# A later lead for the preparation of x, a shorter root for single tiles, and tile 0's root ahead of the weight maxima

## The chip, the cores and the metric

The kernel runs on one core of one Trainium2 chip. The metric is the device time of one execution in microseconds (us); the time shown is the median of three. The core has five engines that work at the same time, each through its own instructions in order: TensorE (PE in the rows; its weight loads are PEld), VectorE (DVE), ScalarE (ACT), GpSimd (POOL) and SyncE (SP), which here only issues DMAs. They wait for each other through semaphores.

## What is computed

One layer of a hybrid encoder over x of 2048 x 1024 (float32):

```
hn = rms_norm(h, norm_w)
proj = hn @ w_in.astype(jnp.float32)
u_f, g_f, q, k, v, g_a = jnp.split(proj, SPLIT_POINTS, axis=-1)
...
f = jnp.fft.fft2(u_f, axes=(1, 3), norm="ortho").real.astype(jnp.float32)
...
o_c, lse_c = dilated_window_attention(q[:, :, sl], k[:, :, sl], v[:, :, sl], window, dilation, slopes)
...
mixed = jnp.concatenate([y_f, y_a], axis=-1) @ w_out.astype(jnp.float32)
h = h + mixed
```

`rms_norm` multiplies each row of x with the reciprocal root of its mean square plus 1e-6 (and with the gain norm_w, which the kernel puts into the weights). The change is in how this first line is prepared.

## The kernel before

**Number format.** Each float32 operand of the projections is split into two fp16 parts, an upper part and a lower part (the remainder). A product of x and a weight is then three products: upper with upper, lower of x with upper of the weight, upper of x with lower of the weight.

**Preparation of x.** x is handled in 16 tiles of 128 rows. Tile r goes through these steps:
- `x_load` (line 173): DMA of 512 KB, issued by SyncE, into `xs`. Tiles 0 to 11 have a place of their own; tiles 12 to 15 take the places of 6 to 9, so their loads wait until tile 6 to 9 is split.
- `x_sq` (line 189): ScalarE squares the tile and adds each row up into `xss`.
- `x_rs` (lines 193 to 200, with `rsqrt_g`, lines 104 to 111): the reciprocal root by an integer start value and three rounds of three small operations on VectorE, each waiting for the one before; 11 links with the mean. Result `xri`. Tiles 0 to 3 have a root of their own (`xn1t` is its scratch), later tiles share one root in pairs (`xn2t`), which needs both tiles' squares.
- `x_hi` (line 212): ScalarE scales the tile and casts it, the upper part (`xhl`).
- `x_lo` (line 220): VectorE computes the lower part from it (also `xhl`).
- Transposition into `xT`. The upper part: 8 transposes on TensorE (`x_tr`, line 227) into PSUM (`xps`) and one copy back (`x_ev`, line 232), on ScalarE for even tiles and on VectorE for odd ones. The lower part: for tiles 0 to 3 the same way with the engines exchanged, from tile 4 on by a DMA transpose that SyncE issues (`x_dt`, line 235).
The upper and lower parts share four buffers (`pp`), so that two tiles can be under way.

**Main loop.** It runs over items: for each of 12 units (two heads of one attention configuration) the projections of 16 tiles, later the other parts of the layer. Step i does item i. The projection of one tile (`inproj`, line 309) is 24 products of 128x128 by 128x384 into one of three PSUM buffers (`psq`); the loop issues them in pieces of 6 among the work of the other engines. The first unit goes through tiles 0 to 15 in steps 0 to 15, so tile r must be ready at step r. In the first products of every tile but tile 0, upper and lower part of x alternate, so the second product already reads the lower part. Three readers on ScalarE empty a finished projection one step later (`q_raw` and `q_v`, lines 320, 321, 328), VectorE follows with line 329 and 339.

**The order is written by hand** (a manual schedule). In step i, in this order: the DMA transposes of the tiles split in the step before (`for r in xd: ... self.x_dt(r)`), the weight loads that fall due (line 245; in steps 3 to 6 two pieces of the next unit's weights, ahead in the program of the DMA transposes of that step), the readers of the step before, the first 6 products, `x_hi` of the tiles named by `xd`, 6 products, the TensorE transposes and copies of the tiles split in the step before (`xt`), `x_lo` of the tiles in `xd` and the loads that need their places, 6 products, the squares, the rest, and at the end of some steps the rest of a root. Between these, `chain` advances by one operation the root of x (`xg`), the roots of the attention's queries and the gains (`gains`, lines 153 to 169, which ends in three DMAs). A generator that is run to its end in a `for _ in xg: pass` is issued in one piece.

**Before the loop.** All loads are issued, the weights of unit 0 first (eight pieces, `wr`); VectorE takes the absolute maximum of each piece (line 261, `w_prep`), the maxima give a power of two as scale (lines 263 to 280), ScalarE and VectorE split the weights with it (lines 286 and 288). The code interleaves `w_prep` (`wg`) with tiles 0 and 1 by `go`, which advances it by one stage.

Of the kernel before, what the change touches and what calls it, by code (L numbers as in the profile page):

```python
# [11 lines left out]
F32 = mybir.dt.float32  # L12
# [3 lines left out]
I32 = mybir.dt.int32  # L16
AF = mybir.ActivationFunctionType
OP = mybir.AluOpType
# [4 lines left out]
S, D = 2048, 1024  # L23
HD = 64
NT = 16
KT = D // 128
EPS = 1e-6
# [62 lines left out]
class Kernel:  # L90
# [100 lines left out]
    def x_rs(self, r0):  # L191
        n = self.xgrp(r0)[1]
        ss = self.XS[r0][:, :n]
        y, g = self.rsqrt_g(ss, n, "xn%d" % n, self.XR[r0][:, :n])

        def gen():
            self.nc.vector.tensor_scalar(ss, ss, 1.0 / D, EPS, op0=OP.mult, op1=OP.add)
            yield
            yield from g
        return gen()  # L200
# [747 lines left out]
    def body(self):  # L948
# [3 lines left out]
        with ExitStack() as ctx:  # L952
# [19 lines left out]
            for _ in range(2):  # L972
                t = self.stp.tile([128, 3, 2, S], F16, name="xs", tag="st", bufs=2)
# [10 lines left out]
            wg = self.w_prep(0)  # L984

            def go(*gs):
                for g in gs:
                    next(g, None)
            self.x_sq(0)
            go(wg, wg)  # L990
            for _ in self.x_rs(0):
                pass
            self.x_hi(0)
            self.x_tr(0, 0)
            go(wg, wg, wg, wg, wg, wg)
            go(wg)
            self.x_lo(0)
            self.x_ev(0, 0)
# [25 lines left out]
            xg = self.x_rs(3)  # L1024
# [32 lines left out]
            xd, xt = [], []  # L1057
            ng = og = iter(())
            self.YD, self.YL = [], []
            for i in range(max(len(items) + 1, G + 32)):  # L1060
                ip, wchunks = iter(()), 0
                if i < len(items):
                    u, _, _, gen, out = items[i]
                    ip = gen() if i else ip0
                    p = i - first[u]
                    if p == 0:
                        wg = iter(())
# [4 lines left out]
                    if p == p0 and u + 1 < NU:  # L1072
                        wg = self.w_prep(u + 1, u + 2 < NU)
# [11 lines left out]
                def chain(k=1):  # L1085
                    for _ in range(k):
                        next(og1, None)
                        next(ng, None)
                        next(xg, None)
                        if 0 < i < NT:  # L1090
                            next(kg, None)
# [26 lines left out]
                if q4:  # L1118
                    self.q_st(*q4)
                chain(1)  # L1120
                xd = [r for r in ([i + 2] if i < 2 else [4, 5] if i == 2 else [i + 3]) if r < NT]
                next(ip, None)
                if b0:
                    self.att_exp(*b0)
# [39 lines left out]
                        self.x_load(r + 6)  # L1164
                chain(2)
                next(ip, None)
                if i < 2:
                    self.x_sq(2 * i + 4)
                    self.x_sq(2 * i + 5)
                elif i + 6 < NT:  # L1170
                    self.x_sq(i + 6)
                chain(1)
                for _ in range(wchunks):
                    next(wg, None)
# [5 lines left out]
                    self.att_o(*ao3)  # L1180
                for _ in og1:
                    pass
                if i % 2 == 0 or i == 1:
                    for _ in xg:
                        pass
                if i == 0:
                    xg = self.x_rs(4)
                if i % 2 and i + 6 < NT:
                    xg = self.x_rs(i + 5)
                if p == count[u] - 1:  # L1190
                    for _ in wg:
                        pass
# [104 lines left out]
```

## Time and profile before

| | |
|---|---|
| time, median of 3 | 1406.22 us |
| lowest and highest of the three | 1406.18 and 1406.72 us |
| time of the profiled execution | 1406.38 us |
| its span, first to last instruction | 1404.6 us |
| mean granted TensorE clock | 0.997 |
| busy: TensorE, VectorE, ScalarE, GpSimd | 98%, 71%, 53%, 33% |

Rows of a timeline have the start of a run of like instructions, its length, engine, line, operation, output and input, the count behind the x, and in brackets how long the engine stood idle ahead of it and what ended that. A length includes the latency of the last instruction, so the pace of a run is better read from starts. In a list of waits a row has who waited for whom, the sum, how many times, and the longest. In the chain of waits a row has the start, the length and what the end of the program waited for at that time.

### The profile page before, as it was taken

To read this page: it belongs to the slowest core of one execution; us is meant where nothing else is said; L and a number is where in the kernel's file an instruction comes from. 1 tells how busy PE (TensorE), PEld (TensorE's weight loads), DVE (VectorE), ACT (ScalarE), POOL (GpSimd) and SP (SyncE) were. 2 spreads that over 40 slices of the span, in tenths; PEclk is the share of its full clock that TensorE was granted. 3 is DMA by queue.
4 is the path that set the end of the run, shared out by engine and by line. 5 is a ranking of instruction groups with operands and counts; after the bars stand their busy time and mean duration, and the time that the engine had idled before them with its cause. 6 is when DMAs were issued, how large, how long until landed. Compare 5 with 4: busy or idle time off the path is not lost.

```text
span 1404.6 us, 27759 instructions
## 1 busy us (share of the span) xinstructions
PE 1373.1 (98%) x9484; PEld 1018.3 (72%) x9484; DVE 996.0 (71%) x3174; ACT 748.9 (53%) x2101; POOL 462.6 (33%) x639
## 2 busy tenths in 40 slices
PE   5999999999999999999999999999999999899998
PEld 3666666667777777778888888844447689688887
DVE  7888888887878888888887777754398877721111
ACT  6867767676766666675756565645213335410010
POOL 0265444444444444454543343321000100411110
PEclk9999999999999999999999999999999999999999
DMA  6977777777776877687766565544423527364342
GB/s 225 205 133 122 153 123 144 124 145 132 138 137 120 151 119 158 116 153 120 142 116 125 103 131 109 128 110 132 168 83 101 155 83 255 91 158 128 112 112 83
DMA packets 426686, 187.62 MB, mean 134 GB/s; under 512 B 320112, under 2 KB 410416, under 8 KB 426032
## 3 DMA queue, kind: packets, MB, share of 16 engines
q1 hardware_dynamic: 397940, 172.84, 56.9%
q10 hardware_dynamic: 28604, 13.00, 4.0%
q8 instruction: 74, 1.21, 0.4%
q14 instruction: 68, 0.56, 0.1%
HBM read 67.65 MB, written 29.76 MB: 69 GB/s over the span
## 4 chain that ended last, share of the span: by engine, by line
PE 82%; DVE 6%; DMA 4%; issue 3%; POOL 2%; ACT 2%; SPq 1%; ACTq 0%; POOLq 0%; DVEq 0%
PE psq L309 44%; PE py L937 13%; PE psq L571 12%; PE psq L587 5%; PE pS L458 3%; PE po L524 2%; PE po L525 1%; DMA Y<-SG 1%; PE pS L446 1%; DVE xhl L220 1%; POOL ph L506 1%; DMA wor<-in_w_out_dram 1%; DMA qw<-qw 1%; DVE wh L288 0%; DMA pt<-ph 0%
## 5 line engine op out<-in xcount | busy, mean ns | idle before, releaser
L309 PE MATMUL psq<-wh,xT 128*128 128x384 f16 x4608 | 787.4, 327 | 3.3 <-ACT wh L286 1.5
L309 PEld LDWEIGHTS <-xT 128*128 128x128 f16 x4608 | 540.6, 119 | 193.9 <-issue 5.1
L494 ACT ACTIVATE P<-pS,ob,kb 128x256 f32<-128x256 f32 (+1 forms) x384 | 199.7, 527 | 150.8 <-DVE ob L486 150.4
L506 POOL TENSOR_TENSOR ph<-P,ph 128x512 f16<-128x512 f32 x160 | 189.3, 1183 | 195.6 <-ACT ph L501 183.3
L937 PE MATMUL py<-wo,mx 128*128 128x512 f32 x768 | 176.5, 392 | 5.9 <-DVE mx L916 4.8
L362 POOL TENSOR_TENSOR qn<-qn,kb 128x128 f32<-128x128 f32 x192 | 85.1, 443 | 294.0 <-DVE qn L361 202.8
L937 PEld LDWEIGHTS py<-wo,mx 128*128 128x128 f32 x768 | 145.4, 190 | 37.1 <-DVE mx L916 5.2
L571 PE MATMUL psq<-xT,wh 128*128 128x512 f16 x768 | 169.0, 379 | 0.0
L476 DVE CUSTOM_DVE_ANT_0 pS<-pS,bt 128x256 f32<-128x256 f32 (+1 forms) x384 | 147.8, 385 | 27.1 <-PE pS L446 18.8
L373 POOL TENSOR_TENSOR hl<-qn,hl 128x256 f16<-128x256 f32 x192 | 134.3, 699 | 30.6 <-ACT hl L368 30.6
L571 PEld LDWEIGHTS <-wh 128*128 128x128 f16 x768 | 74.1, 98 | 87.1 <-issue 0.8
L940 DVE TENSOR_TENSOR xo<-xo,py 128x512 f32<-128x512 f32 x32 | 22.0, 688 | 139.6 <-PE py L937 139.6
L535 DVE TENSOR_REDUCE ob<-po 128x128 f32<-128x256 f32 (+1 forms) x160 | 75.2, 470 | 53.9 <-PE po L525 53.9
L501 ACT CAST ph<-P 128x512 f16<-128x512 f32 x160 | 99.1, 619 | 8.7 <-DMA wr<-in_w_in_dram 1.7
L368 ACT CAST hl<-qn 128x256 f16<-128x256 f32 x192 | 77.1, 401 | 47.3 <-POOL qn L362 37.5
L329 DVE TENSOR_TENSOR vt<-psq,vt 128x128 f16<-128x128 f32 x192 | 55.0, 286 | 60.7 <-ACT vt L328 60.6
L328 ACT CAST vt<-psq 128x128 f16<-128x128 f32 x192 | 51.3, 267 | 82.9 <-PE po L525 82.9
L288 DVE SCALAR_TENSOR_TENSOR wh<-wr,nws,wh 128x384 f16<-128x384 f32 x128 | 87.5, 690 | 7.1 <-ACT wh L286 7.1
L587 PE MATMUL psq<-wh,xT 128*128 128x256 f16 x768 | 84.3, 273 | 0.0
L587 PEld LDWEIGHTS <-xT 128*128 128x128 f16 x768 | 75.1, 98 | 9.1
L915 ACT CAST mx<-ya 128x512 fp32r<-128x512 f16 x16 | 9.9, 620 | 134.5 <-PE py L937 127.8
L320 ACT COPY raw<-psq 128x256 f32<-128x256 f32 x192 | 69.6, 362 | 21.6 <-PE psq L309 21.2
(158 smaller groups left out, 1770.8 us busy)
## 6 DMA issues: line engine op xcount, KB each, us to landing
wr<-in_w_in_dram SPq DMA_DIRECT2D x104, 192.0 KB, 3.0
ot<-O SPq DMA_DIRECT2D x16, 792.0 KB, 4.6
st<-st SPq DMA_DIRECT2D x96, 128.0 KB, 2.4
xs<-in_x_dram SPq DMA_DIRECT2D x16, 512.0 KB, 7.2
xo<-in_x_dram SPq DMA_DIRECT2D x16, 512.0 KB, 3.7
out_dram<-xo SPq DMA_DIRECT2D x15, 512.0 KB, 3.0
O<-ob ACTq DMA_DIRECT2D x108, 66.0 KB, 2.6
O<-ob ACTq DMA_DIRECT2D x32, 132.0 KB, 3.1
```

Of the source, the lines that this page charges most:

```text
L288: V.scalar_tensor_tensor(wh[:, 1, k - 1, :n], wr[k - 1], nws[:, k - 1:k], wh[:, 0, k - 1, :n], op0=OP.mult, op1=OP.subtract)
L309: nc.tensor.matmul(ps[:, :384], self.xtile(j, k, c, t), wh[:, l, k, :384], start=n == 0, stop=n == 23)
L362: G.tensor_tensor(qn[:, 2:4], qn[:, 2:4], self.kf[:, h0:h0 + 2], OP.mult)
L368: self.nc.scalar.copy(hl.rearrange("p a h l d -> p (a h) l d")[:, :, 0], qn)
L373: self.nc.gpsimd.tensor_tensor(hv[:, :, 1], qn, hv[:, :, 0], OP.subtract)
L476: V.tensor_tensor_reduce(out=sS[:, h, cs], in0=ps[:, h, cs], in1=bs, scale=1.0, scalar=-3.0e38, op0=OP.add, op1=OP.max, accum_out=mx[:, e, ...
L494: self.nc.scalar.activation(P[:, h, cs], sS[:, h, cs], AF.Exp, bias=ob[:, e, 130 + h:131 + h], scale=self.om[:, h0 + h:h0 + h + 1], accum_ ...
L501: self.nc.scalar.copy(ph[:, 0], P)
L506: self.nc.gpsimd.tensor_tensor(ph[:, 1], P, ph[:, 0], OP.subtract)
L571: nc.tensor.matmul(ps, wh[:, l, k, col * 128:col * 128 + 128], self.xT[:, j, k, ch * 512:ch * 512 + 512], start=n == 0, stop=n == 23)
L587: nc.tensor.matmul(ps[:, j * 256:j * 256 + 256], self.xT[:, i, k, r * 128:r * 128 + 128], wh[:, l, k, 128:384], start=n % 24 == 0, stop=n ...
L937: nc.tensor.matmul(ps[nh], m[:, j, k], wo[nh][k][:, l], start=(j, l, k) == (0, 0, 4), stop=(j, k) == (1, 3))
```

## The change

1. **A root of its own form for single tiles.** `x_rs` of tiles 0 to 3 takes the mean with a factor of -1/2 in the first operation, a start value for that, and then three rounds of two operations instead of three: 8 links instead of 11. The roots of pairs keep their form.
2. **Tile 0's root ahead of the maxima.** Before the loop, two maxima stood between the square and the root of tile 0; they now follow it with the other six.
3. **The lead.** Which tiles are split in step i (`xd`) was tile 2 in step 0, tile 3 in step 1, tiles 4 and 5 in step 2 and tile i + 3 from then on. Now it is tile i + 2 in steps 0 to 3, tiles 6 and 7 in step 4 and tile i + 3 from then on.
4. **The squares** were two a step in steps 0 and 1 (tiles 4 to 7) and one a step from then on (tile i + 6). Now they are one a step in steps 0 to 3 (tile i + 4), two in steps 4 and 5 (tiles 8 to 11), and tile i + 6 from then on.
5. **The roots of pairs.** The root of 4 and 5 was spread over step 1 (from the end of step 0, with the rest in one piece at its end). Now the roots of 4 and 5, 6 and 7, 8 and 9 are issued in one piece at the end of steps 1, 3 and 4; that of 10 and 11 is spread from step 5 on as before.

```diff
@@ x_rs
+        if n == 1:
+            y = self.XR[r0][:, :1]
+            t = self.sm.tile([128, 1], F32, name="xnt", bufs=3)
+
+            def gen1():
+                V.tensor_scalar(ss, ss, -0.5 / D, -0.5 * EPS, op0=OP.mult, op1=OP.add)
+                yield
+                V.tensor_scalar(y.bitcast(I32), ss.bitcast(I32), -0.5, float(0x5F3759DF - 2 ** 30 - 2 ** 22), op0=OP.mult, op1=OP.add)
+                yield
+                for _ in range(3):
+                    V.scalar_tensor_tensor(t, y, ss, y, op0=OP.mult, op1=OP.mult)
+                    yield
+                    V.scalar_tensor_tensor(y, t, 1.5, y, op0=OP.add, op1=OP.mult)
+                    yield
+            return gen1()
@@ before the loop
             self.x_sq(0)
-            go(wg, wg)
             for _ in self.x_rs(0):
                 pass
             self.x_hi(0)
             self.x_tr(0, 0)
-            go(wg, wg, wg, wg, wg, wg)
+            go(wg, wg, wg, wg, wg, wg, wg, wg)
@@ step i
-                xd = [r for r in ([i + 2] if i < 2 else [4, 5] if i == 2 else [i + 3]) if r < NT]
+                xd = [r for r in ([i + 2] if i < 4 else [6, 7] if i == 4 else [i + 3]) if r < NT]
...
-                if i < 2:
-                    self.x_sq(2 * i + 4)
-                    self.x_sq(2 * i + 5)
-                elif i + 6 < NT:
-                    self.x_sq(i + 6)
+                for r in [i + 4] if i < 4 else [8, 9] if i == 4 else [10, 11] if i == 5 else [i + 6]:
+                    if r < NT:
+                        self.x_sq(r)
...
-                if i % 2 == 0 or i == 1:
+                if i % 2 == 0:
                     for _ in xg:
                         pass
-                if i == 0:
-                    xg = self.x_rs(4)
-                if i % 2 and i + 6 < NT:
-                    xg = self.x_rs(i + 5)
+                if i in (1, 3, 4, 5) or i % 2 and i + 6 < NT:
+                    xg = self.x_rs(2 * i if i == 4 else i + 3 if i < 4 else i + 5)
+                    if i < 5:
+                        for _ in xg:
+                            pass
```

The change moves lines of the file down by 16, so line 212 of before is line 228 after it, and so on.

**ScalarE, from tile 2's upper part on.** `xjk` is a square, `raw`, `sq` and `vt` are the readers of a projection, `xhl` an upper part, `xT` a copy of transposes. Before:

```order
L212 ACTIVATE xhl_325<-xs_107,xri_281 128x1024
L189 ACTIVATE xjk_337,xss_335<-xs_107 128x1024
L189 ACTIVATE xjk_339,xss_335<-xs_107 128x1024
L320 COPY raw_346<-psq_253 128x256
L321 ACTIVATE sq_347<-psq_253 128x256
L328 CAST vt_350<-psq_253 128x128
L212 ACTIVATE xhl_364<-xs_107,xri_314 128x1024
L232 COPY xT_106<-xps_384 128x8x128
L189 ACTIVATE xjk_421,xss_419<-xs_108 128x1024
L189 ACTIVATE xjk_423,xss_419<-xs_108 128x1024
```

And after:

```order
L228 ACTIVATE xhl_316<-xs_107,xri_275 128x1024
L189 ACTIVATE xjk_328,xss_326<-xs_107 128x1024
L336 COPY raw_331<-psq_247 128x256
L337 ACTIVATE sq_332<-psq_247 128x256
L344 CAST vt_335<-psq_247 128x128
L228 ACTIVATE xhl_348<-xs_107,xri_305 128x1024
L248 COPY xT_106<-xps_364 128x8x128
L189 ACTIVATE xjk_397,xss_326<-xs_107 128x1024
```

One square stands ahead of the readers instead of two, and one behind the copy of tile 2.

**VectorE, from tile 3's lower part on.** `xhl` is the lower part, `kt` are the last operations of the gains, `xss`, `xri` and `xn2t` the root of tiles 4 and 5. Before:

```order
L220 SCALAR_TENSOR_TENSOR xhl_365<-xs_107,xri_314,xhl_364 128x1024
L107 TENSOR_TENSOR xn2t_345<-xri_336 128x2
L163 TENSOR_SCALAR kt_141<-kt_141,kinv_355 24x1
L164 TENSOR_SCALAR kt_141<-kt_141 24x1
L165 TENSOR_SCALAR kt_141<-kt_141 24x1
L109 SCALAR_TENSOR_TENSOR xn2t_345<-xn2t_345,xss_335 128x2
L111 SCALAR_TENSOR_TENSOR xri_336<-xn2t_345,xri_336 128x2
```

And after (two more rounds of the last three rows follow):

```order
L236 SCALAR_TENSOR_TENSOR xhl_349<-xs_107,xri_305,xhl_348 128x1024
L163 TENSOR_SCALAR kt_141<-kt_141,kinv_339 24x1
L164 TENSOR_SCALAR kt_141<-kt_141 24x1
L165 TENSOR_SCALAR kt_141<-kt_141 24x1
L213 TENSOR_SCALAR xss_326<-xss_326 128x2
L104 TENSOR_SCALAR xri_327<-xss_326 128x2
L107 TENSOR_TENSOR xn2t_405<-xri_327 128x2
L109 SCALAR_TENSOR_TENSOR xn2t_405<-xn2t_405,xss_326 128x2
L111 SCALAR_TENSOR_TENSOR xri_327<-xn2t_405,xri_327 128x2
```

The whole root of tiles 4 and 5 stands behind tile 3's lower part, where before its first five links stood ahead of it.

**SyncE, from tile 4's DMA transpose on.** The four DMA transposes are those of tiles 4, 5, 6 and 7; `xs` are the loads of tiles 12 and 13, `wr` pieces of the next unit's weights. Before:

```order
L235 DMA_TRANSPOSE xT_106<-xhl_452 128x8x128
L235 DMA_TRANSPOSE xT_106<-xhl_455 128x8x128
L173 DMA xs_108<-in_x_dram 128x1024
L245 DMA wr_579<-in_w_in_dram 128x3x128
L245 DMA wr_581<-in_w_in_dram 128x3x128
L235 DMA_TRANSPOSE xT_106<-xhl_533 128x8x128
L173 DMA xs_108<-in_x_dram 128x1024
L245 DMA wr_655<-in_w_in_dram 128x3x128
L245 DMA wr_657<-in_w_in_dram 128x3x128
L235 DMA_TRANSPOSE xT_106<-xhl_600 128x8x128
```

And after:

```order
L251 DMA_TRANSPOSE xT_106<-xhl_432 128x8x128
L261 DMA wr_544<-in_w_in_dram 128x3x128
L261 DMA wr_546<-in_w_in_dram 128x3x128
L251 DMA_TRANSPOSE xT_106<-xhl_498 128x8x128
L173 DMA xs_108<-in_x_dram 128x1024 x2
L261 DMA wr_628<-in_w_in_dram 128x3x128
L261 DMA wr_630<-in_w_in_dram 128x3x128
L251 DMA_TRANSPOSE xT_106<-xhl_564 128x8x128
L251 DMA_TRANSPOSE xT_106<-xhl_567 128x8x128
```

Two weight loads stand between the transposes of tiles 4 and 5, and both loads of x ahead of tile 6's transpose, where before one stood ahead of tile 6's and one ahead of tile 7's.

## Rows read from the trace of the kernel before

**Rows 1.** The summary of the page: busy time of each engine, its share of the span and its instructions, and the chain that ended last by engine.

```profile
PE 1373.1 (98%) x9484; PEld 1018.3 (72%) x9484; DVE 996.0 (71%) x3174; ACT 748.9 (53%) x2101; POOL 462.6 (33%) x639
...
PE 82%; DVE 6%; DMA 4%; issue 3%; POOL 2%; ACT 2%; SPq 1%; ACTq 0%; POOLq 0%; DVEq 0%
```

**Rows 2.** The list of waits of TensorE, the first 300 us: who waited for whom, us in total, times, longest.

```profile
PE xps L227 <- ACT xhl L212: 10.2, 1, 10.2
PE psq L309 <- ACT wh L286: 1.5, 2, 1.1
...
PE psq L309 <- ACT xT L232: 1.5, 2, 0.8
...
PE xps L227 <- DVE xhl L220: 0.4, 1, 0.4
PE psq L309 <- DVE xT L232: 0.2, 1, 0.2
```

**Rows 3.** The timeline of TensorE from 0 to 110 us (x24 are 24 products of one or two tiles, line 227 are transposes).

```profile
31.59 0.34 PE L309 MATMUL psq<-wh,xT 128*128 128x384 f16 x1 [0.83 <-ACT xT L232]
32.09 1.96 PE L309 MATMUL psq<-wh,xT 128*128 128x384 f16 x11 [0.16 <-DVE xT L232]
...
37.68 1.96 PE L309 MATMUL psq<-wh,xT 128*128 128x384 f16 x11 [0.62 <-ACT xT L232]
...
40.37 4.09 PE L309 MATMUL psq<-wh,xT 128*128 128x384 f16 x24
...
44.74 4.06 PE L309 MATMUL psq<-wh,xT 128*128 128x384 f16 x24
48.65 0.61 PE L227 MATMUL xps<-idh,xhl 128*128 128x128 f16 x8
49.09 4.06 PE L309 MATMUL psq<-wh,xT 128*128 128x384 f16 x24
```

**Rows 4.** The timeline of all engines from 0 to 40 us: the root of tile 0, the other six maxima, the upper part of tile 0, and the upper part of tile 2.

```profile
6.90 0.14 DVE L197 TENSOR_SCALAR xss<-xss 128x1 f32<-128x1 f32 x1
...
8.90 3.09 DVE L261 TENSOR_REDUCE am<-wr 128x1 f32<-128x384 f32 x6
9.01 1.15 ACT L212 ACTIVATE xhl<-xs,xri 128x1024 f16<-128x1024 f32 x1 [3.21 <-DVE xri L111]
...
25.67 1.15 ACT L212 ACTIVATE xhl<-xs,xri 128x1024 f16<-128x1024 f32 x1
```

**Rows 5.** The chain of waits from 0 to 16 us.

```profile
7.18 4.22 DMA wr<-in_w_in_dram
...
11.43 0.56 DVE am L261
```

**Rows 6.** The timeline of all engines from 0 to 40 us again, around tiles 2 to 4.

```profile
28.80 0.35 ACT L320 COPY raw<-psq 128x256 f32<-128x256 f32 x1
...
29.48 1.16 ACT L212 ACTIVATE xhl<-xs,xri 128x1024 f16<-128x1024 f32 x1
...
30.53 1.01 ACT L232 COPY xT<-xps 128x1024 f16<-128x1024 f16 x1
...
31.36 0.67 DVE L232 COPY xT<-xps 128x1024 f16<-128x1024 f16 x1
31.42 1.07 ACT L189 ACTIVATE xjk<-xs 128x1024 f16<-128x1024 f32 x1
...
32.47 1.06 ACT L189 ACTIVATE xjk<-xs 128x1024 f16<-128x1024 f32 x1
...
34.35 0.16 DVE L111 SCALAR_TENSOR_TENSOR xri<-xn2t,xri 128x2 f32<-128x2 f32 x1
...
36.64 0.99 ACT L232 COPY xT<-xps 128x1024 f16<-128x1024 f16 x1
```

**Rows 7.** From the views of line 235 (the DMA transposes of lower parts), the time from issue to landing: of the one issued at 37.60 alone, and then of all twelve up to 90 us.

```profile
DMA to landing us min/median/max: 4.9/4.9/4.9
...
DMA to landing us min/median/max: 4.2/4.6/5.1
```

**Rows 8.** The timeline of SyncE's queue from 0 to 60 us, and ahead of it VectorE's subtraction for tile 6.

```profile
41.36 1.28 DVE L220 SCALAR_TENSOR_TENSOR xhl<-xs,xri,xhl 128x1024 f16<-128x1024 f32 x1
...
37.60 3.70 SPq L235 DMA_TRANSPOSE xT<-xhl  x2
...
43.07 0.96 SPq L245 DMA_DIRECT2D wr<-in_w_in_dram  x2
44.08 1.67 SPq L235 DMA_TRANSPOSE xT<-xhl  x1
...
47.29 2.13 SPq L245 DMA_DIRECT2D wr<-in_w_in_dram  x2
```

**Rows 9.** Three stretches late in the program, of line 937's products alone (busy us and count of each engine, then the granted clock, the DMA share and GB/s), and ahead of them TensorE's longest wait after its first instruction.

```profile
PE py L937 <- DVE mx L916: 4.8, 1, 4.8
...
1225.05:1235.00 9.95, 9.95 (x35) 8.05 (x36) 0.80 0.71 146
1240.00:1250.00 10.00, 10.00 (x46) 8.29 (x45) 1.00 0.36 100
```

More of the change, by code (lines that the diff above doesn't have):

```diff
@@ L193, in x_rs @@
         ss = self.XS[r0][:, :n]
+        V = self.nc.vector
+        if n == 1:
[12 more added lines that the diff above has]
+            return gen1()
         y, g = self.rsqrt_g(ss, n, "xn%d" % n, self.XR[r0][:, :n])
```

## The prediction, made before the changed kernel ran

> **What bounds the kernel now.** First the summary of the page: TensorE is busy 98% of the span, and the chain that ended last is 82% TensorE [rows 1]. So the list of what TensorE waited for says what a change outside TensorE can win [rows 2]. This one touches nothing behind tile 15 of x, so only the waits of the first 75 us count: 10.2 us for the first upper part, then pieces that sum to 1.5 us and less. TensorE's own work shows where they lie [rows 3]: tile 2's first two products wait 0.83 and 0.16 us (31.59, 32.09), tile 3's second one 0.62 us (37.68). From there to tile 6 and beyond it has no gap, and 24 products and 8 transposes repeat every 4.35 us (44.74, 49.09), 3.91 for the products (44.74 to 48.65) and 0.44 for the transposes. The run of 24 at 49.09 is 12 of tile 5 and 12 of tile 6, so tile 6's first product starts at 49.09 + 12 x 0.163 = 51.04. Its second, the first that reads the lower part, starts at 51.20. Up to there both programs do the same products and transposes (tiles up to 7 are transposed), and behind it TensorE's work is the same. **What the changed kernel makes of 51.20 is the whole effect**, unless a later tile comes late too.
>
> **Tile 0's root ahead of the maxima: 0.** Two maxima (6 take 3.09 us, so 0.515 each) stand no longer ahead of the root, which starts at 6.90 - 1.03 = 5.9 and has 8 links of 0.192 us instead of 11 (6.90 to 9.01), so the upper part starts at 7.4 instead of 9.01 [rows 4]. But tile 0's products need the scale of the weights, and that needs all eight maxima. The eighth starts at 11.43, when its weights have landed (7.18 + 4.22 = 11.40) [rows 5]. Eight maxima from 7.4 on reach the eighth at 11.0, and it then waits for the same landing. Only 8 transposes come earlier. What hides the gain is that landing; without it 1.6 us would be won.
>
> **Shorter roots of tiles 1 to 3: 0.2 to 0.3 by themselves.** Three links less are 0.58 us each. Tile 1's lower part is the one that TensorE waited for, 0.4 us [rows 2]; that bounds the gain, and the upper part of tile 1, which is ScalarE's, leaves 0.3 of it. Tile 2's upper part moves from 25.67 to 25.2: ScalarE's square ahead of it is now last, not the root.
>
> **One square a step instead of two: 1.5 in all at tile 2.** On ScalarE from start to start a square takes 1.05 us, the three readers of a projection 0.68, an upper part 1.05, a copy 0.89 [rows 6]. Tile 2's subtraction ends 0.5 sooner, at 27.6, with three links of tile 3's root behind it, so that root ends at 28.1. One square less stands ahead, so ScalarE is free by then: tile 3's upper part goes from 29.48 to 28.1, tile 2's copy from 30.53 to 29.15, ending at 30.15. VectorE's copy of tile 2 stood 1.88 us behind the end of that root (29.48 to 31.36), four links of the pair's root among it; without them 1.6, so 29.7, ending at 30.4. TensorE reaches tile 2 at 31.59 - 0.83 - 0.3 = 30.45. Both waits go: the second product at 30.6 instead of 32.09. Gain 1.5, the 0.3 within it.
>
> **What is late next: tile 4's root.** Before, it was interleaved and ended with the link at 34.35 [rows 6]. Now it is issued in one piece behind VectorE's copy, tile 3's subtraction (to 31.55) and the last gain operations (to 31.9): 11 links of 0.192 end at 34.0. ScalarE has waited for it since 31.8. Tile 4's upper part starts at 34.0; the copy of tile 3's lower part stands behind it on ScalarE, 35.05 to 36.05 (before 36.64 to 37.63). Tile 3's second product goes at 36.1 instead of 37.68: gain 1.55, with a new wait of 0.7 in place of the 0.62.
>
> **Tiles 4 and 5.** Tile 4's subtraction ends at 36.4 and its DMA transpose goes at 36.4 instead of 37.60. That one took 4.9 us to land [rows 7, 8], so 41.3. TensorE stands there from 40.3 and continues at 41.3, where before it was at 40.37 + 13 x 0.163 = 42.49 [rows 3]; but tile 5's transposes, 0.44, are still due. Tile 5 has its upper part at 37.7, its subtraction from 38.85 to 40.05, the transpose at 40.1, landed by 45.0 and needed at 45.7: in time. Net gain so far 0.75: TensorE would be at tile 6 at 51.04 - 0.75 = 50.3.
>
> **Tile 6 decides.** The pair that builds up the lead is now 6 and 7. Their root needs the square of tile 7, which ScalarE reaches at 39.6, one after the other from 34.0 (upper part, copy, square, readers, upper part, copy); done at 40.8. The root ends at 42.9, the upper parts start at 42.9 and 44.0. VectorE copies tile 5 (44.0), subtracts for tile 6 (44.6) and 7 (45.8), and ends at 47.1. Two things follow.
> ScalarE's copy of tile 6 stands behind the upper part of tile 8, and that behind the root of 8 and 9, issued in one piece behind tile 7's subtraction: 47.5 + 2.1 = 49.7, upper part to 50.75, copy to 51.75. Tile 6's first product, due at 50.3, goes at 51.8.
> On SyncE the loads of tiles 12 and 13 now stand ahead of tile 6's transpose, and the second needs the end of tile 7's subtraction; two weight loads follow. Before, a load of x and two of weights took the time from the subtraction's end (41.36 + 1.28 = 42.64) to the transpose at 44.08, 1.44 us [rows 8]. The same behind 47.1 gives 48.5: 4.4 us later. Landing takes 4.2 to 5.1 us [rows 7]; between two loads of x and two of weights I take the median, 4.6: 53.1. The second product goes at 53.1 instead of 51.20: **1.9 us lost**.
> Bounds: 4.2 and a chain 0.5 us quicker than mine give 52.2, 1.0 lost; 5.1 and 0.4 of delay give 54.0, 2.8 lost. Tile 7 has landed by 55 and is needed at 57.4. Tile 8's subtraction needs tile 6's buffer (53.1), so its transpose goes near 55.8 and lands by 60.9; needed at 61.8. From there the lead is the old one. TensorE has no slack to take the shift back.
>
> **Sum.** -1.55 at tile 3, +0.36 at tile 4's landing, +0.44 of transposes still due: -0.75. TensorE's wait at tile 6 is then 53.1 - 50.45 = 2.65: +1.9. The profiled execution took 1406.38 with its span of 1404.6; 1406.38 + 1.9 = 1408.3. The median shown lies 0.16 below that execution: **1408.1 us**, 0.13% more. A measurement of this kernel tells about 0.2%, 2.8 us, from no change, so this counts as no change.
>
> **Rivals.** (1) *The lead suffices:* the chain from 34.0 to 47.1 is over 1.2 us quicker than I laid it, so that tile 6's copy and transpose come in time (transpose at 46.2 or before). TensorE keeps up to 0.75: 1405.5 to 1407.2. For it: small links overlap well with others in these rows. Against it: the two loads of x stand ahead of the transpose however quick VectorE is. A gain of over 2.8 us would need nearly all of TensorE's waits behind the first, 1.5 + 1.5 + 0.4 + 0.2 [rows 2].
> (2) *SyncE's queue makes it worse:* of the pairs of weight loads one held the queue for 2.13 us instead of 0.96 [rows 8]. Ahead of tile 6 that puts its transpose at 49.7; with 5.1 it lands at 54.8, 3.6 lost: 1409.8. From a landing at 54.0 on, the kernel is slower by more than 0.2%.
> (3) *The clock falls:* after TensorE's one wait of 4.8 us, near 1225 us, the granted clock is 0.80 and 35 products start in the 9.95 us in which 46 are usual at 1.00 [rows 9], a loss of 2.3 us. After 0.83 us eleven products took 1.96 us, the level of 2.4 GHz [rows 3]. My wait, broken by one product, lies between: 1408.1 + 2.3 = 1410.4.
> The Trainium skill ("TensorE: Matmul & The Clock Gate", section "Why this matters for your kernels") warns that gaps between bursts of matmuls put the engine back to its low level. The row at 1225 agrees; by the page a wait like mine may or may not be long enough, and no row here shows one.
>
> **Chances and range.** Forecast (1407.2 to 1409.0) 0.63, rival 1 0.13, rival 2 0.17, rival 3 0.05, a gain over 0.2%, of which I see no source, 0.02. So slower by over 0.2% 0.23 (rivals 2 and 3 and the forecast's upper edge), faster 0.02, within 0.75. The range goes from 1405.8, into rival 1, to 1409.9, the price of rival 2; about 0.15 is left out.
>
> **What would show it.** Right: new waits of TensorE for tile 6 between 50 and 54 us, on ScalarE's copy and then on the DMA transpose; none at tile 2; tile 4's upper part waits about 2 us for its root; tile 6's transpose goes near 48.5; the eighth maximum starts at 11.4 as before. Wrong: that transpose goes by 46.2, or lands before TensorE asks; the products of tile 0 start before 15.0; a wait at tile 8 or later, which would add to the loss.

## The result, and the profile after

| | before | changed |
|---|---|---|
| median, first set of runs | 1406.2 us (4 runs) | 1413.0 us (4 runs, 1412.14 to 1414.35) |
| profiled execution, its span | 1406.38, 1404.6 | 1413.57, 1411.8 |
| mean granted TensorE clock | 0.997 | 0.995 |

The ratio is 1.005, with a 95% interval of 1.0037 to 1.0062: the changed kernel is slower by about half a per cent. Two more sets of runs, on other occasions, gave 1411.4 and 1412.2 us (ratios 1.0034 and 1.0041). The forecast was 1408.1 us and the range ended at 1409.9. One of the twelve executions of experiment 1 took 2922.6 us and is left out of its time and its ratio.

The timeline of TensorE in the changed kernel, around tiles 2 to 8 (lines are 16 higher than before; L325 is the projection, L243 the transposes). It answers to [rows 3].

```profile
28.71 4.13 PE L325 MATMUL psq<-wh,xT 128*128 128x384 f16 x24
...
36.56 1.96 PE L325 MATMUL psq<-wh,xT 128*128 128x384 f16 x11 [0.67 <-ACT xT L248]
...
41.62 1.96 PE L325 MATMUL psq<-wh,xT 128*128 128x384 f16 x11 [0.54 <-DMA xT<-xhl]
...
48.66 2.12 PE L325 MATMUL psq<-wh,xT 128*128 128x384 f16 x12
52.39 0.34 PE L325 MATMUL psq<-wh,xT 128*128 128x384 f16 x1 [1.62 <-ACT xT L248]
56.40 3.70 PE L325 MATMUL psq<-wh,xT 128*128 128x384 f16 x11 [3.67 <-DMA xT<-xhl]
59.89 1.06 PE L243 MATMUL xps<-idh,xhl 128*128 128x128 f16 x8
60.74 4.70 PE L325 MATMUL psq<-wh,xT 128*128 128x384 f16 x24
...
65.73 4.07 PE L325 MATMUL psq<-wh,xT 128*128 128x384 f16 x24
```

Up to 48.66 it goes much as forecast: 24 products in one run at 28.71, where tile 2 had two waits, 0.67 in place of the 0.62 at tile 3, and 0.54 for tile 4's DMA transpose. Then two large waits for tile 6 with one product between them. Tile 6's second product goes at 56.40 instead of 51.20 [rows 3], 5.20 later. And the eleven products behind the wait take 3.70 where eleven took 1.96 at 41.62: by 65.73 (57.78 before) the lag has grown to 7.95. The stretches below (busy time and count of TensorE, then the granted clock, the DMA share and GB/s) say why: within the second wait, near 55 us, the clock fell to its lower level, 1.2 GHz (0.50 granted), and it came back to 1.00 near 62 us.

```profile
50.00:55.00 5.00, 1.11 (x6) 1.00 1.15 198
55.00:60.00 5.00, 3.60 (x13) 0.52 1.10 282
60.00:65.00 5.00, 5.00 (x32) 0.80 1.08 216
```

What made the wait stands in SyncE's queue, against [rows 8], and in the view of line 251 for the one transpose issued at 49.21 (its length as an instruction, then its landing), against [rows 7]:

```profile
46.46 1.69 SPq L173 DMA_DIRECT2D xs<-in_x_dram  x2
48.21 0.96 SPq L261 DMA_DIRECT2D wr<-in_w_in_dram  x2
49.21 5.93 SPq L251 DMA_TRANSPOSE xT<-xhl  x2
```

```profile
L251 SPq DMA_TRANSPOSE xT<-xhl x1: 3849/3849/3849, 49.2 to 49.2; - x1
...
DMA to landing us min/median/max: 7.1/7.1/7.1
```

Two loads of x and two of weights, 1.4 MB, are issued within 2.75 us. Tile 6's transpose follows at 49.21. Its issue holds SyncE for 3.85 us, where tile 4's took 1.35, and it lands 7.1 us after its start: 3.2 us after the issue was through. The six other traces with this order (experiments 3, 8, 9, 12, 14 and 15) have landings of 6.8 to 7.6 us. The issue took 3.7 to 4.3 us in five of them, but 2.0 in 15, which landed in 6.8 all the same; so the late landing does not hang on a long issue. ScalarE shows the first of the two waits (start, length, and what ended the idle time):

```profile
34.46 1.15 ACT L228 ACTIVATE xhl<-xs,xri 128x1024 f16<-128x1024 f32 x1 [2.05 <-DVE xri L111]
...
50.29 1.15 ACT L228 ACTIVATE xhl<-xs,xri 128x1024 f16<-128x1024 f32 x1 [1.82 <-DVE xri L111]
51.35 0.99 ACT L248 COPY xT<-xps 128x1024 f16<-128x1024 f16 x1
```

At 34.46 tile 4's upper part has waited 2.05 us for its root; at 50.29 that of tile 8 has, and tile 6's copy stands behind it.

Not all of the 7.95 us reaches the end. The kernel before had two waits further on, which the changed kernel has no more, since TensorE comes later and everything is ready (timeline of TensorE, kernel before, with the next run behind them, then the same run in the changed kernel):

```profile
72.18 0.49 PE L267 MATMUL pm<-idf,am 128*128 128x128 f32 x2 [0.22 <-DVE am L264]
...
119.73 0.49 PE L458 MATMUL pS<-st 128*128 128x256 f16 x3 [0.88 <-DMA st<-st]
...
124.95 4.06 PE L309 MATMUL psq<-wh,xT 128*128 128x384 f16 x24
```

```profile
131.37 4.06 PE L325 MATMUL psq<-wh,xT 128*128 128x384 f16 x24
```

Behind them the lag is 6.42 us, so 1.5 came back. The start, 0.33 later in this execution because the weights landed later, stands in the 5.20 already. So 5.20 + 2.75 - 1.5 = 6.4; the rest of the 7.2 us by which the spans differ came between 450 and 720 us, in small waits of TensorE.

### The profile page after: what moved, and what is told of

The parts are those of the page before. It is cut to its first block, busy times and chain, and to the rows that moved or that the text cites. A ratio compares the mean times of both kernels' runs of the same rounds, so it can differ in the third digit from the quotient of the medians.

```text
span 1411.8 us, 27745 instructions
## 1 busy us (share of the span) xinstructions
PE 1375.9 (97%) x9484; PEld 1019.0 (72%) x9484; DVE 995.0 (70%) x3162; ACT 748.8 (53%) x2101; POOL 461.0 (33%) x639
## 3 DMA queue, kind: packets, MB, share of 16 engines
q8 instruction: 74, 1.21, 0.4%
## 4 chain that ended last, share of the span: by engine, by line
PE 86%; DMA 4%; DVE 4%; issue 2%; ACT 1%; POOL 1%; SPq 1%; POOLq 0%; DVEq 0%; ACTq 0%
PE psq L325 47%; PE py L953 12%; PE psq L587 12%; PE psq L603 5%; PE pS L474 3%; PE po L540 2%; PE po L541 1%; PE pf L837 1%; DMA Y<-SG 1%; PE pS L462 1%; DMA pt<-ph 1%; DMA wr<-in_w_in_dram 1%; DMA qw<-qw 1%; DMA xT<-xhl 1%; POOL ph L522 0%
## 5 line engine op out<-in xcount | busy, mean ns | idle before, releaser
L325 PE MATMUL psq<-wh,xT 128*128 128x384 f16 x4608 | 790.3, 328 | 8.2 <-DMA xT<-xhl 4.2
L325 PEld LDWEIGHTS <-xT 128*128 128x128 f16 x4608 | 541.2, 119 | 200.7 <-issue 7.3
L345 DVE TENSOR_TENSOR vt<-psq,vt 128x128 f16<-128x128 f32 x192 | 54.8, 286 | 63.6 <-ACT vt L344 63.5
```

The source lines that it names most:

```text
L325: nc.tensor.matmul(ps[:, :384], self.xtile(j, k, c, t), wh[:, l, k, :384], start=n == 0, stop=n == 23)
```

## The experiments

Each was timed in turn with the kernel before on the same chip; the kernels within a set (1 to 4, 5 to 7, 8 to 11, 12 to 15) share its runs: 1406.22, 1406.24, 1406.92 and 1406.06 us.

**1. Parts one and two alone** (shorter root, tile 0's root first; lead, squares and later roots as before):

```diff
+        if n == 1:
+            y = self.XR[r0][:, :1]
...
+            return gen1()
...
             self.x_sq(0)
-            go(wg, wg)
...
-            go(wg, wg, wg, wg, wg, wg)
+            go(wg, wg, wg, wg, wg, wg, wg, wg)
```

> The kernel before with only the shorter root of single tiles and tile 0's root ahead of the maxima; the lead stays as it was. Theory (the whole loss comes from the later lead): the upper part of tile 0 starts near 7.4 us, the eighth maximum still waits for its weights, tile 2 and tile 3 gain a few tenths at most: 1405.8 to 1406.3 us. Rival (these two parts cost something too): 1407 us or more, with a wait at tile 0, 1 or 2 that the kernel before has not.

1406.42 us, ratio 1.0001 (0.9993 to 1.001): no difference. The time is 0.1 above the theory's bracket, but below the rival's. Tile 2's two waits stay (0.83 and 0.16). TensorE is 0.63 ahead at 57.15, and at 72.41 it is 0.2 behind: waits for ScalarE (0.17 at 70.07) and VectorE (0.74 at 72.41) took it back, and the wait for a DMA near 120 us is there as before (0.91 at 119.99). The loss is the later lead's.

**2. The loads of x a step later:**

```diff
                 for r in xd:
                     if r > 3:
                         self.x_dt(r)
+                for r in xl:
+                    self.x_load(r)
+                xl = []
...
-                        self.x_load(r + 6)
+                        xl.append(r + 6)
```

> The changed kernel with the loads of tiles 12 to 15 of x issued a step later, behind the DMA transposes of that step; nothing else moves. Theory (the megabyte of x ahead of tile 6's transpose made it late, and the long wait made the clock fall): the transpose goes near 46.5 us, lands by 51.5, TensorE waits once for tile 6, for ScalarE's copy until 52.4, the granted clock stays at 1.00: 1407.0 to 1408.0 us. Rival (the later lead itself is too short, whatever the queue holds): tile 6 or tile 7 still waits for its transpose until 54 us or more, 1410 us or more.

1407.65 us, 1.0008 (0.9999 to 1.0016), as the theory had it. SyncE's queue and TensorE:

```profile
45.90 2.95 SPq L251 DMA_TRANSPOSE xT<-xhl  x2
48.94 1.01 SPq L173 DMA_DIRECT2D xs<-in_x_dram  x2
```

```profile
51.75 2.12 PE L325 MATMUL psq<-wh,xT 128*128 128x384 f16 x12 [1.43 <-ACT xT L248]
```

The transpose goes 3.3 us sooner and is no more waited for; nothing was issued close ahead of it, since the two weight loads, which no longer stand behind a load of x that waits for VectorE, went at 41.40. Where the trace shows a landing of these transposes up to 60 us, it took 3.6 to 4.7 us. One wait is left at tile 6, for ScalarE's copy; the clock stays at 1.00. Two more follow, for tile 11's upper part (0.55 at 71.81) and the maxima (0.68 at 74.09): the lag is 0.7 at tile 8 and 1.9 behind them. So what stood ahead of this transpose in SyncE's queue made 3 to 5 of the 4.5 to 6.8 us by which the changed kernel was slower in its three sets; 1.4 are left.

**3. Dummy products in the wait.** 22 products, then tile 6's first:

```diff
+                if i == 6:
+                    dm = self.psm.tile([128, 512], F32, name="dm", tag="m")
+                    for k in range(22):
+                        nc.tensor.matmul(dm[:, :384], self.xtile(0, k % KT, 0, 5), self.W[0][0][:, 0, k % KT, :384], start=k == 0, stop=k == 21)
                 next(ip, None)
```

> The changed kernel with 22 products added ahead of tile 6's first one, into a PSUM tile that nobody reads, so that TensorE works from 50.8 to 54.4 us where it waited. Everything else stays, the late transpose too (second product of tile 6 at 56.4). Theory (the fall of the granted clock is 2.5 to 2.8 us of the loss by itself): the products behind 56.4 go at full pace, 1410.0 to 1410.8 us. Rival (the slow products behind the wait are something else, such as VectorE or ScalarE holding their buffers): 1412.5 us or more.

1411.75 us, 1.0041 (1.0029 to 1.0053): between the two. In its trace the clock holds at 1.00 behind a wait of 2.20 us, the eleven products take 1.96 again, and from tile 6's second product to the run that was at 65.73 it takes 6.59 us instead of 9.33. But the time is still 5.5 us above the kernel before, and the changed kernel's three sets are 6.8, 4.5 and 6.2 above it: of these 2.7 us little or nothing is seen at the end; 9 and 12 to 15 follow this up.

**4. The lead where it was, squares spread, roots in one piece:**

```diff
-                xd = [r for r in ([i + 2] if i < 4 else [6, 7] if i == 4 else [i + 3]) if r < NT]
+                xd = [r for r in ([i + 2] if i < 2 else [4, 5] if i == 2 else [i + 3]) if r < NT]
...
-                for r in [i + 4] if i < 4 else [8, 9] if i == 4 else [10, 11] if i == 5 else [i + 6]:
+                for r in [4] if i == 0 else [5, 6] if i == 1 else [7, 8] if i == 2 else [i + 6]:
...
-                if i in (1, 3, 4, 5) or i % 2 and i + 6 < NT:
-                    xg = self.x_rs(2 * i if i == 4 else i + 3 if i < 4 else i + 5)
-                    if i < 5:
+                if i in (1, 2) or i > 2 and i % 2 and i + 6 < NT:
+                    xg = self.x_rs(4 if i == 1 else 6 if i == 2 else i + 5)
+                    if i < 3:
```

> The changed kernel with the lead built up where it was, by tiles 4 and 5, but the squares spread (4; 5 and 6; 7 and 8; then one a step) and the roots of 4 and 5 and of 6 and 7 in one piece at the end of their steps. Theory (the loss comes from where the pair stands, not from roots in one piece): no wait at tile 6, tile 2's two waits gone, 1405.0 to 1406.4 us. Rival (roots in one piece hold up ScalarE's upper parts wherever they stand): 1408 us or more, with ScalarE waiting about 2 us for a root ahead of tile 4 and TensorE behind it.

1407.17 us, 1.0004 (0.9995 to 1.0012), between the two brackets. There is no wait at tile 6, so the place of the pair decides. But nothing is won either: ScalarE waits 0.96 us for the pair's root, and what tile 2 gains, tile 3 pays:

```profile
37.88 1.96 PE L325 MATMUL psq<-wh,xT 128*128 128x384 f16 x11 [1.64 <-ACT xT L248]
```

**5. As 2, and tile 6's copy ahead of tile 8's upper part:**

```diff
                 for r in xd:
-                    self.x_hi(r)
+                    if i != 5:
+                        self.x_hi(r)
...
                 for r in xd:
+                    if i == 5:
+                        self.x_hi(r)
                     self.x_lo(r)
```

> The changed kernel with the loads of x a step later (as in the second experiment) and, in step 5, ScalarE's copy of tile 6 ahead of the upper part of tile 8. Both theories expect tile 6's first two products near 50.4 us, 1.3 us sooner than in the second experiment, without a wait of more than 0.5 us there. Theory (TensorE has later waits, on tile 11's upper part near 71 us, the weight maxima near 73 and the queries' transpose near 120, that end when the other engines are done, and these swallow what is won ahead of them): those waits grow from 1.9 to 3 us together, and the time stays at 1407.2 to 1407.7 us. Rival (TensorE is the bound all through, so that what is won at tile 6 is won at the end): 1406.0 to 1406.6 us.

1406.82 us, 1.0004 (0.9995 to 1.0012), between the brackets again. TensorE has no wait at tile 6 and is 1.0 us ahead of the kernel before at tile 8 (56.78 against 57.78). Then:

```profile
70.83 0.62 PE L243 MATMUL xps<-idh,xhl 128*128 128x128 f16 x8 [1.29 <-ACT xhl L228]
...
73.17 0.49 PE L283 MATMUL pm<-idf,am 128*128 128x128 f32 x2 [0.74 <-DVE am L280]
```

The lead over the kernel before is gone by 73.17: that one was there at 72.18, 1.0 sooner. Of the 1.7 us that this kernel gained over experiment 2 by tile 8, 0.9 is left there, and 0.8 in the medians: TensorE's early waits are in part only moved.

**6. In the kernel before, only tile 6's transpose a step later**, just ahead of tile 7's:

```diff
-                for r in xd:
+                for r in dl + xd:
                     if r > 3:
-                        self.x_dt(r)
+                        if r == 6 and i == 4:
+                            dl = [6]
+                        else:
+                            self.x_dt(r)
+                            if i == 5:
+                                dl = []
```

> The kernel before with one thing changed: the DMA transpose of tile 6 is issued a step later, just ahead of tile 7's, behind one load of x and two of weights. Theory (a late transpose of tile 6 alone makes the loss): issued near 49.5 us, landed 4.2 to 4.9 us later, TensorE waits 2.5 to 3.2 us in one piece ahead of tile 6's second product; with the granted clock at 1.00 behind it and up to 1.1 us given back at the later waits 1407.6 to 1409.0 us, with a fall of the clock 1410.0 to 1411.5 us. Rival (the changed kernel loses elsewhere, and a late transpose alone is taken up by the slack): 1406.0 to 1406.8 us.

1407.66 us, 1.0009 (1.0001 to 1.0018). Timelines of SyncE and TensorE:

```profile
48.92 3.06 SPq L235 DMA_TRANSPOSE xT<-xhl  x2
```

```profile
52.98 1.96 PE L309 MATMUL psq<-wh,xT 128*128 128x384 f16 x11 [1.66 <-DMA xT<-xhl]
```

The late transpose makes a loss by itself: 1.4 us in the medians (0.1 to 2.5 by the interval), 1.8 at tile 6's second product (52.98 against 51.20). In this execution 0.5 of it is left by 154 us, so how much of the 1.4 is the transpose's stays open. The wait was 1.66 and not 2.5, mostly since the two weight loads held the queue for 1.60 and not 2.13. Behind one load of x and two of weights it landed in 4.0 us: issued 0.3 us earlier than in the changed kernel, it was there 3.4 us earlier. So a late issue alone costs 1.8 of the 5.2 us at this product; the larger part came with the second load of x, issued 1.2 us behind the first.

**7 and 10. The weight loads of steps 3 to 6 behind the transposes;** 1.0 MB of x stays ahead. 10 is the same kernel again.

```diff
-                    if u == 0 and 3 <= p < 7:
-                        for k in range(2 * p - 6, 2 * p - 4):
-                            self.w_load(1, k)
...
                         self.x_dt(r)
+                if 3 <= i < 7:
+                    for k in range(2 * i - 6, 2 * i - 4):
+                        self.w_load(1, k)
```

> The changed kernel with the weight loads of steps 3 to 6 behind the DMA transposes of their step; the two loads of x stay ahead of tile 6's transpose, 1.0 MB instead of 1.4. Theory (the transpose is served when what was queued ahead of it has moved, at 300 to 360 GB/s): issued near 48.2 us, landing in 5.8 to 6.8 us, tile 6's second product at 54.0 to 55.0; 1408.5 to 1410.0 us if the granted clock holds. Rival (the landing is the usual 4.2 to 5.1 us from the issue, and 7.1 was chance): second product at 52.4 to 53.3, 1407.0 to 1408.3 us.

> The kernel of the seventh experiment once more, for a second profile, since its profiled execution was the quickest of its six by 2 us. Theory (the usual execution waits longer for tile 6's transpose than that one did): landing in 5.8 us or more, tile 6's second product at 53.5 or later, 1409.5 to 1412 us. Rival (it lost its time elsewhere): second product at 52.4 to 53.0 again, and the time lost behind 75 us.

7: 1410.87 us, 1.0032 (1.002 to 1.0044), its profiled execution 1407.54. 10: one run, 1411.41. TensorE in the two:

```profile
51.59 0.34 PE L325 MATMUL psq<-wh,xT 128*128 128x384 f16 x1 [2.13 <-ACT xT L248]
52.67 3.33 PE L325 MATMUL psq<-wh,xT 128*128 128x384 f16 x11 [0.75 <-DMA xT<-xhl]
```

```profile
52.25 0.34 PE L325 MATMUL psq<-wh,xT 128*128 128x384 f16 x1 [2.13 <-ACT xT L248]
54.39 3.70 PE L325 MATMUL psq<-wh,xT 128*128 128x384 f16 x11 [1.80 <-DMA xT<-xhl]
```

Issued at 47.24 and 47.97, the transpose was used 5.4 and 6.4 us later: more than the usual landing, less than 7.1, and different from one execution to the next by 1 us. Its own issue took only 1.30 and 1.48. Both times the clock fell (to 0.50 granted), though the waits were 2.13 and 0.75, and 2.13 and 1.80, with a product between. The median is above both brackets of 7, because that fall was not in them.

**8 and 11. The changed kernel again, and with four weight loads ahead,** 1.8 MB in all:

```diff
-                    if u == 0 and 3 <= p < 7:
-                        for k in range(2 * p - 6, 2 * p - 4):
+                    if u == 0 and 3 <= p < 6:
+                        for k in range(2 * p - 6, 2 * p - 4 if p < 5 else 8):
```

> The changed kernel itself, beside the two that follow on the same chip. Expected: 1412.0 to 1413.5 us, with the wait of 1.6 us, one product, the wait of 3.7 us and a granted clock near 0.5 between 55 and 62 us.

> The changed kernel with the two weight loads of step 6 issued in step 5 already, so that two loads of x and four of weights, 1.8 MB instead of 1.4, stand ahead of tile 6's transpose. Theory (it is served when what was queued ahead has moved): landing not before 57.3 us, tile 6's second product 0.9 to 1.6 us later than in the changed kernel, 0.8 to 1.6 us more in all. Rival (7.1 us has another cause, such as two loads of x waiting for VectorE): second product within 0.5 us of the changed kernel's, the same time.

8: 1411.38 us, 1.0034 (1.0022 to 1.0047). 11: 1413.55 us, 1.0048 (1.0034 to 1.0062). The rows of tile 6's transpose in the two, and in the changed kernel's other two sets (the first, and experiment 15 below):

| | first load of x | transpose issued | issue took | issue ended, from the first load | landed, from its issue | tile 6's second product, from tile 0's first |
|---|---|---|---|---|---|---|
| first set | 46.46 | 49.21 | 3.85 | 6.60 | 7.1 | 40.88 |
| 8 | 45.97 | 48.56 | 4.11 | 6.70 | 7.3 | 40.94 |
| 15 | 46.13 | 48.75 | 2.02 | 4.64 | 6.8 | 40.41 |
| 11 | 46.29 | 49.95 | 4.08 | 7.74 | 6.7 | 41.35 |

With 0.38 MB more ahead, the issue is through 1.04 us later than in 8, as the theory says; but in 15, the same kernel as 8, it is through 2.06 sooner, so one trace of each does not show it. The second product goes 0.75 later than in 8 (56.70 against 55.95), less than its bracket and more than the rival's, and 0.41 later if counted from tile 0's first product. So the theory is not borne out: it needs the landing to follow the bytes one for one, and 0.38 MB less (7 and 10) made it shorter, but 0.38 MB more made it no longer. That loads issued just ahead make the landing late is shown by 2, 6, 7 and 10 together; whether their bytes, their number or the late second load of x count was not separated. The times differ by more than either expected, and their intervals overlap.

**9. 33 dummy products,** enough to fill the whole wait (as 3, with 33).

> The changed kernel with 33 products ahead of tile 6's first one, into a PSUM tile that nobody reads, enough to fill TensorE's time until tile 6's transpose has landed. Theory (the fall of the granted clock costs 2.7 us, as the two traces have it from tile 6's second product to tile 7's): 2.2 to 3.0 us below the changed kernel of this call. Rival (the trace of one execution says too much; what the clock costs is mostly given back later): 0.3 to 1.5 us below it.

1412.96 us, 1.0042 (1.003 to 1.0055): not below the changed kernel at all. Both expectations failed. Yet in the trace the clock holds, and at 427 us this kernel is 2.0 us ahead of 8; by 731 us they are level. Either the later waits had taken the gain, or the added products cost something.

**12 to 15. Controls on one chip.** The 33 products stand ahead of tile 0's first transposes instead, where TensorE waits anyway, in the changed kernel (12) and in the kernel before (13); 14 is 9 again, 15 the changed kernel.

```diff
             self.x_hi(0)
+            dm = self.psm.tile([128, 512], F32, name="dm", tag="m")
+            for k in range(33):
+                nc.tensor.matmul(dm[:, :128], self.idh, self.idh, start=k == 0, stop=k == 32)
             self.x_tr(0, 0)
```

> The changed kernel with 33 unread products of 128 columns ahead of the first transposes, in the time in which TensorE waits for tile 0 anyway; the wait at tile 6 and the fall of the clock stay. Theory A (the added products cost something far behind, which hid what the held clock saved in the ninth experiment): 1.0 to 2.5 us above the changed kernel of this call. Theory B (they cost nothing, and the late waits between 420 and 730 us take back what the held clock saved): within 0.7 us of it.

> The kernel before with the same 33 early products. Theory A: 1407.2 to 1408.7 us. Theory B: 1405.8 to 1406.8 us.

> The kernel of the ninth experiment beside the changed kernel and the control on the same chip. If the held clock is worth its 2.7 us at the end: 2.0 to 3.0 us below the control with early products. If not: within 1.2 us of it.

> The changed kernel itself, for the three above: 1411.3 to 1413.5 us.

| | median | ratio to before (interval) |
|---|---|---|
| 12 changed, early products | 1414.71 | 1.0058 (1.0046 to 1.0071) |
| 13 before, early products | 1408.30 | 1.0016 (1.0007 to 1.0025) |
| 14 changed, wait filled | 1412.64 | 1.0045 (1.0031 to 1.0058) |
| 15 changed | 1412.22 | 1.0041 (1.0029 to 1.0054) |

Theory A holds. 33 unread products cost 2.2 us in the kernel before and 2.5 in the changed one, and not where they stand: tile 0's first products go at 15.21 in 13, 15.19 in the kernel before. They cost it between 430 and 740 us, in TensorE's waits for the attention's DMA transposes. The lists of waits of that stretch, of the kernel before and of 13, then of 15 and of 12:

```profile
PE po L524 <- DMA pt<-ph: 0.6, 1, 0.6
```

```profile
PE po L524 <- DMA pt<-ph: 3.6, 3, 1.6
```

```profile
PE po L540 <- DMA pt<-ph: 0.4, 1, 0.4
```

```profile
PE po L540 <- DMA pt<-ph: 4.0, 4, 1.5
```

That this is the added products' doing, and not the chance of one execution, is seen over all traces: this sum is 3.0 to 4.0 us in the four with 33 products (9, 12, 13 and 14), and 0.3 to 1.6 in the thirteen others, 1.4 in 3 among them.

So the fair comparison for the clock is 14 against 12, both with 33 added products (of 384 and of 128 columns): 2.07 us less, in the bracket of 2.0 to 3.0. The traces of the two agree: from tile 6's second product to the run of 24 that was at 65.73, 14 takes 6.59 us and 12 takes 8.46, 1.87 more. The lower mean clock of 12 (0.990) is no rival: it stems from the time before 25 us, where the clock is shown as 0.50 in 12 and as 1.00 in 13, at the same pace: the eight transposes near 13.5 us take 1.03 and 1.04 us. And of the eleven executions of 13 the five with a mean of 0.991 or 0.992 have a median of 1407.93 us, no more than the others. The held clock is worth about 2 us of the loss.

## Why the prediction was wrong

- **Tile 0's root ahead of the maxima: 0.** Right. The upper part starts at 7.41 (7.4 forecast, in part by luck: the root started 0.2 sooner than assumed, at 5.69, and its 8 links took 1.7 us, not 1.54), the eighth maximum still waits for its weights (11.76, idle 0.79 ahead of it), and experiment 1 shows no difference.
- **Shorter roots and one square a step: 1.5 at tile 2.** Right: 1.21 by 32.68 against 33.89, plus the 0.33 of the later start. **Tile 4's root late.** Right: 34.46 (34.0 forecast), tile 3's second product 36.56 (36.1), the new wait 0.67 (0.7).
- **Tiles 4 and 5.** Right: tile 4's second product 41.62 (41.3), tile 5 in time.
- **Tile 6, the copy and the issue.** Right within what was foreseen: first product 52.39 (51.8), transpose issued 49.21 (48.5), both with that 0.33 in them.
- **Tile 6, the landing: 4.6 us.** This is the step that failed. It was the median of landings that had at most one load of x close ahead; the prediction saw two loads of x and two of weights in the queue and priced the time that SyncE needs to issue them, but nothing for what they do to the transfer behind them. It took 7.1 (6.8 to 7.6 in experiments 3, 8, 9, 12, 14 and 15), 2.5 more, and landed at 56.3, not 53.1. With nothing close ahead (2) the wait for it goes, with 0.9 MB (6) it lands in 4.0, with 1.0 MB in two loads of x (7 and 10) it is used after 5.4 and 6.4. This is rival 2, the queue, but not by its path: the transpose was not issued at 49.7 to land in 5.1, at 54.8; the landing itself was longer.
- **The clock.** Rival 3, at 0.05, came about. Its price there, 2.3, was near: 2.07 between 14 and 12, and 2.75, 2.59 and 2.22 in the three traces of the changed kernel (first set, 8 and 15). It should not have stood apart at 0.05: a longer landing brings it along, and in 7 it came with waits of 2.13 and 0.75, hardly more than the broken wait of 2.65 that was forecast. The Trainium skill ("TensorE: Matmul & The Clock Gate", section "Why this matters for your kernels") warns of gaps between bursts; the trace agrees, with a granted clock of 0.52 from 55 to 60 us, around the end of the wait of 3.67 us, and 1.00 behind single waits of 2.20 (experiment 3) and 1.66 (6). In 10, as in 7, the clock fell with no single wait above 2.13 us, but two with one product between.
- **"TensorE has no slack to take the shift back."** Wrong by 1.5 us, which the waits at 72.18 and 119.73 gave back. The first of them and the one for tile 11's upper part explain why 1 and 5 win nothing: TensorE comes sooner and waits there. In 4 the wait at tile 3 took the gain.

So the forecast's 1.9 became 5.2 - 0.33 = 4.9, by the landing (2.5) and an issue 0.4 later than forecast; 7.6 by the clock; and about 6.1 by what was given back. The medians say 4.5 to 6.8. No version tried beats the kernel before. What stays open: what in the loads ahead sets the landing, how the added products reach the attention's transposes, and why 5 is still 0.6 above the kernel before, within its interval. In its trace 5 is level with that kernel up to 1180 us; then a wait for VectorE (line 808, 792 before) takes 1.6 us where it took 0.6.

## What to carry to other kernels

A load that is issued just ahead of a transfer in the same queue can make that transfer land later, here by 2.5 us, and not only be issued later: ask of every moved step which transfers now stand ahead of the one that TensorE needs next, and put those with a later due time behind it. Price a wait and the clock together, since a long wait, or two with little work between them, is what let the clock fall here. And in a list of TensorE's waits look at the next ones down the line before you book a gain: they often hold what an early wait gave up.

## What the hardware showed that was not expected

The issue of DMA transposes is itself held behind queued loads. A single one took 1.2 to 2.0 us in the kernel before. Those of tiles 6 and 7, one behind the other, held SyncE for 5.6 to 6.4 us together with 1.4 or 1.8 MB issued just ahead (eight traces), 4.2 and 5.3 with 1.0 MB (7 and 10), 3.1 with 0.9 (6) and 3.0 with nothing close ahead (2); all that SyncE would issue next is held with them. How the hold is shared between the two differs: 3.85 and 2.04 us in the first set, 2.02 and 3.49 in 15.

The granted clock does not tell the pace of TensorE's first work. In 13 the 33 early products of 128 columns took 3.70 us, 0.112 each, with the clock shown as 1.00; from 43.42 to 43.87 in the changed kernel eight transposes of the same shape took 0.45, 0.056 each. The eight near 13.5 us took 1.03 us in 12, with the clock shown as 0.50, and 1.04 in 13, with 1.00.

Some 33 products that nobody reads and that delay nothing near them cost 2.2 us 400 us later. The sum of the waits for one kind of transfer there went from 0.6 to 3.6 us, and it is 3.0 us or more in every trace with 33 of them and 1.6 or less in every other; by which path was not found.
